# Gate and up of a gated MLP turned token-major, in eleven groups with two of eight weight pieces by seven products

## Chip, core and metric

The kernel runs on one core of a Trainium2 chip. The metric is the device time of one execution in microseconds (us). Engines: TensorE (PE in the profile; PEld its weight loads), VectorE (DVE), ScalarE (ACT), GpSimd (POOL) and SyncE (SP), which issues the loads.

## What is computed

One layer of a bidirectional encoder over 256 tokens with 2048 features: norm, two attention branches with gates, output projection, a gated MLP with a convolution of width 3 along the tokens, a gated per-layer embedding, norm. The part that matters here is the MLP, with 5632 inner columns:

```python
hf = rms_norm(x, ffn_norm[i])
g = dwconv_centred(hf @ w_ffn_gate[i], conv_w[i], conv_b[i])
x = x + (jax.nn.gelu(g) * (hf @ w_ffn_up[i])) @ w_ffn_down[i]
```

## The kernel before

**Precision.** Every fp32 operand of a product is split into a high half, rounded to fp32r, and a low half, the rest. A product is three matmuls (`thirds`, lines 361 to 366): high by high, high by low, low by high. The split of a weight is made on the chip: ScalarE rounds the raw weights (L263), VectorE subtracts (L264).

**Pieces and units.** The weights come in pieces of 128 x 2048 numbers, 1 MB each, in the order of use (`_pieces`); SyncE loads them into three buffers. `produce` cuts a piece into units of up to 1024 columns and splits them. There are rings for six plain units (`uh`, `ul`) and two units of differences (`vh`, `vl`); a new unit is made when the products that read an old one are issued (`drop`, `pump`), strictly in the order of `_UNITS`. So VectorE can be about two to three pieces ahead.

**Two ways to use a piece token-major.** In the stages B (branch gates), D (output projection), F (down) and G (embedding gate) the moving operand is weights, 128 x 512, and the stationary one 128 x 128 of activations. A piece holds two row blocks by two blocks of 512 columns; the activations are two row blocks by two halves of 128 tokens. A piece of kind `s` makes the eight products, 24 matmuls. A piece of kind `S` makes seven products, as in Winograd's form of Strassen's method, 21 matmuls. It needs two units of weight differences (T13 and T24; L256 to L258 make the differences on VectorE in the raw buffer, then they are split) and four sums of activations, made once per pair of row blocks (`sums_of`, L835 to L841). The products of an S piece come in the order M1, M7, M5, M6, M2, M3, M4; M7 and M5 need T13, M6 and M4 need T24. Each name is one of the eight PSUM banks; the eighth, P22, is used by s pieces and for transposes. `row_sums` joins the banks at the last piece of a stage: one copy on ScalarE and four adds of 512 columns on VectorE (L810 to L814), then for each of four blocks `finish`.

**Feature-major.** In E (gate and up) the weights are the stationary operand, 128 x 128, and the moving one is `hf`, 128 x 512: the high and low halves of 256 tokens. A block is a matmul of 512 (L307) and one of 256 with the low weights (L314), written as sixteen and sixteen (`unit_blocks`). There are 44 columns of 128 for gate and as many for up, half of them in E0 and half in E1. `mlp` (L962) does the rest for each column, on 128 x 256: the halves' sum (`gather`), the norm's scale, the three taps with a `tensor_scalar` and two `scalar_tensor_tensor` (L970 to L972), gelu by tanh, the product with up, the split of the result, and for five pairs of columns a half the sums for S pieces. The scale by the norm is a row spread over all partitions (`norm_columns`, one matmul).

**Stages.** E0, F00, F01, E1, F10, F11: F00 and F01 make the two halves of the 2048 output columns from E0's rows of activation, F10 and F11 from E1's. Each F stage has eleven pieces of the pattern `SsSsSsSsSss`, so F0 and F1 have 22 each. F's `finish` adds to the residual (L924, L926). In F11 the finished rows are turned back by transposes (`rows_pair`, L858) for the next stage, and two `combine` make activation sums. Behind F11 come pp0 and pp1 (one s piece each) and G.

**Order.** `at((stage, piece, product), f)` hangs work at a place of TensorE's program; the framework then orders the instructions of every engine with its own estimate of their times, mostly by their place in the program. Engines run their lists in order.

Of the kernel before, what the change touches and what calls it, by code (L numbers as in the profile page):

```python
# [16 lines left out]
P = 128  # L17
# [14 lines left out]
FC = FF // P  # L32
FHALF = FC // 2
EPS = 1e-6
# [53 lines left out]
WARM = 14  # L88
JOINT = 4
JOINED = 2  # L90
# [3 lines left out]
ALT = "SsSsSsSs"  # L94
DOWN = "SsSsSsSsSss"
FIRST_GATES = "ssssSsSs"


def _ffn(half):

    jobs = []
    for f in range(FHALF + 1):
        if f < FHALF:
            jobs.append(("g", half * FHALF + f))
        if f:
            jobs.append(("u", half * FHALF + f - 1))
    return jobs


def _pieces():  # L110
# [27 lines left out]
    for s in range(2):  # L138
        quads("D%d" % s, ("w_out", 2 * s * WIDE), ("w_out", (2 * s + 1) * WIDE), ALT)
    for half in range(2):  # L140
        names = {"g": "w_ffn_gate", "u": "w_ffn_up"}
        jobs = [(names[kind], f) for kind, f in _ffn(half)]
        joint = 0 if half else JOINT
        e = [(name, k, f) for k in range(KC) for name, f in jobs[:joint]]
        e += [(name, k, f) for name, f in jobs[joint:] for k in range(KC)]
        blocks("E%d" % half, e)
        for s in range(2):
            quads("F%d%d" % (half, s), ("w_ffn_down", 2 * s * WIDE), ("w_ffn_down", (2 * s + 1) * WIDE),
                  DOWN, half * FHALF)
    for s in range(2):  # L150
# [32 lines left out]
_EARLY = [0] + list(np.cumsum([_LAST_OF[u] + 1 for u in range(40)]))  # L183
RINGS = {"u": 6, "v": 2}


@with_exitstack
def _encoder(ctx: ExitStack, tc, xt, pt, xrow, cols, gainrow, table, onehot, mask, ident_in, wts, out):
# [9 lines left out]
    BANK = {"M2": 0, "M3": 1, "M4": 2, "M1": 3, "M7": 4, "M5": 5, "M6": 6, "P22": 7}  # L198
    RING = {"acc": (0, 1, 2), "sp": (3, 4), "pt": (5, 6), "misc": (7,), "e": (0, 1, 2, 3, 5, 6, 4)}
    turns = {"acc": 1}  # L200
# [241 lines left out]
    def gather(acc, scale=1.0, u=None, keep=lambda ins: ins):  # L442

        t = sc.tile([P, T], F32, name="t")
        keep(nc.scalar.activation(t, acc[:, T:], AF.Copy, scale=scale))  # L445
        if u is None:
            u = sc.tile([P, T], F32, name="u")
# [32 lines left out]
    def diagonal(r):  # L480

        dg = sc.tile([P, T], F32, name="rdg", bufs=1)
        for t in range(2):
            nc.vector.tensor_scalar(dg[:, t * P:(t + 1) * P], ident, r[:, t:t + 1], None, op0=ALU.mult)
        return dg

    def spread(key, dg):

        b = bank("misc", P, T)
        nc.tensor.matmul(b, ones, dg, start=True, stop=True)  # L490
        rt[key] = sc.tile([P, T], F32, name="rms", bufs=1)
        nc.scalar.activation(rt[key], b, AF.Copy)
# [337 lines left out]
    def sums_of(u, tag):  # L830

        tok = held["tok"]
        f = tok.tile([P, 4, P], F32, name="cmb")
        x11, x21, x12, x22 = (u[:, k, t * P:(t + 1) * P] for k in range(2) for t in range(2))
# [11 lines left out]
    def combine(key, m, pair, tag):  # L846

        u = held["tok"].tile([P, 2, T], F32, name="pair", bufs=2)
# [100 lines left out]
    residual("D1", 1, lambda k: held["merged"][:, k, :], "merged", True)  # L949
    for pair, which in enumerate(("M2", "M3", "M4", "P22")):  # L950
        at(("E0", 2 + pair), rows_pair, which, 4 + pair, hf, 1)

    def norm_columns():
        at(("E0", 11), spread, 1, diagonal(rows_root()))

    at(("E0", 8), norm_columns)

    def activation_row(k):
        k %= FHALF
        return held["act"][1][k - 16] if 16 <= k < 20 else held["act"][k // 20 * 2][:, k - k // 20 * 20, :]  # L960

    def mlp(kind, n, acc):  # L962
        tok = held["tok"]
        if kind == "g":
            if n % 2 == 0:
                held["gw"] = tok.tile([P, 4, T], F32, name="gw", tag="c%d" % (n // 2 % 2 + 1))
            c, w = (held["gw"][:, 2 * (n % 2) + i] for i in range(2))
            u = gather(acc)
            nc.vector.tensor_tensor(u, u, rt[1], op=ALU.mult)
            nc.vector.tensor_scalar(c, u, tap(1, n), tap(3, n), op0=ALU.mult, op1=ALU.add)  # L970
            nc.vector.scalar_tensor_tensor(c[:, 1:], u[:, :-1], tap(0, n), c[:, 1:], op0=ALU.mult, op1=ALU.add)
            nc.vector.scalar_tensor_tensor(c[:, :-1], u[:, 1:], tap(2, n), c[:, :-1], op0=ALU.mult, op1=ALU.add)  # L972
            nc.scalar.activation(w, c, AF.Square)
            nc.vector.tensor_scalar(w, w, 0.044715, 1.0, op0=ALU.mult, op1=ALU.add)
            nc.vector.tensor_tensor(w, w, c, op=ALU.mult)
            nc.scalar.activation(w, w, AF.Tanh, scale=GELU_C)
            nc.vector.scalar_tensor_tensor(c, w, 1.0, c, op0=ALU.add, op1=ALU.mult)
            held["gelu", n] = c
        else:
            if n % 2 == 0:  # L980
                held["pair"] = tok.tile([P, 2, T], F32, name="pair", bufs=2)
            u = gather(acc, u=held["pair"][:, n % 2])
            nc.vector.scalar_tensor_tensor(u, u, 0.5, rt[1], op0=ALU.mult, op1=ALU.mult)
            nc.vector.tensor_tensor(u, u, held.pop(("gelu", n)), op=ALU.mult)
            halves(activation_row(n), u)
            pair = n % FHALF // 2
            if n % 2 and DOWN[pair] == "S":
                combos["act", pair] = sums_of(held["pair"], pair // 2)

    ph_, pl_ = [], []  # L990

    def load_last():
        held["pr"] = held["tok"].tile([P, 2, T], F32, name="pair", bufs=2)
        keep(nc.sync.dma_start(held["pr"], pt))

    def split_last():
        for k in range(2):
            ph_.append(sc.tile([P, T], FR, name="t"))
            pl_.append(sc.tile([P, T], FR, name="u"))
            nc.scalar.activation(ph_[k], held["pr"][:, k], AF.Copy)  # L1000
            nc.vector.tensor_tensor(pl_[k], held["pr"][:, k], ph_[k].bitcast(F32), op=ALU.subtract)

    for half in range(2):
        held["act"] = [big.tile([P, 16, 2 * T], FR, name="act", tag="R1"),
                       [big.tile([P, 2 * T], FR, name="act1", tag="yb%d" % i) for i in range(4)],
                       held["tok"].tile([P, 2, 2 * T], FR, name="act2")]
        jobs = _ffn(half)
        joint = 0 if half else JOINT
        stage = "E%d" % half
        accs = [bank(which) for which in ("M1", "M5", "M6", "M7")[:joint]]  # L1010
        if joint:
            products(stage, lambda k: hf[:, k, :], KC, accs)
        for (kind, n), a in zip(jobs, accs):
            mlp(kind, n, a)
        turns["e"] = 0
        for kind, n in jobs[joint:]:
            mlp(kind, n, product(stage, lambda k: hf[:, k, :], KC, "e"))
        if half:
            at(("F10", 2, 0), load_last)
            at(("F10", 9, 0), split_last)  # L1020
            held["ssq"] = sc.tile([P, 2, 2], F32, name="ssq", bufs=1)
        residual("F%d0" % half, 0, activation_row, "act", half)
        if half:
            pl = big.tile([P, KC, 2 * T], FR, name="pl", tag="R0")
            for pair, when in enumerate((("F11", 0, 6), ("F11", 1, 2), ("F11", 1, 5), ("F11", 2, 1))):
                at(when, rows_pair, "P22", pair, pl, 2)
            at(("F11", 2, 4), combine, "pl", pl, 0, 0)
            at(("F11", 4, 4), combine, "pl", pl, 2, 1)
        residual("F%d1" % half, 1, activation_row, "act", half)
# [4 lines left out]
    gains = last[:, 2 * D:]  # L1034
    nc.sync.dma_start(gains, gainrow)
    for pair, which in enumerate(("M2", "M3", "M4", "P22")):
# [5 lines left out]
    at(("pp1", 0, 0), ple_root)  # L1042
    at(("pp1", 0, 4), combine, "pl", pl, 4, 2)
    at(("G0", 1, 4), combine, "pl", pl, 6, 3)
    names = ("M1", "M6", "M7", "M5")

    class Rows:
# [3 lines left out]
        def __getitem__(self, i):  # L1051
            c = i[1]
            h = (ph_, pl_)[c.start >= T][self.k]
            return h[:, c.start % T:c.start % T + P]

# [109 lines left out]
```

## Time and profile before

| | us |
|---|---|
| median of 3 runs (1457.73 to 1458.08) | 1457.87 |
| the profiled execution | 1458.43 |
| its span from first to last instruction | 1456.6 |
| E0, F0, E1, F1 of it | 247.1, 113.0, 244.9, 114.5 |

Loads move 282.88 MB, 194 GB/s on the mean. The page gives busy times by engine, the chain of waits that ended last, and groups of instructions by line. The windows table gives for each stretch its length and the busy time of each engine in it; the timeline lists instructions with start and duration, "x3" for three in a row, and in brackets how long the engine was idle before them and what ended that.

### The profile page before, as it was taken

Reading aid. Unit: us, or ns where it says so; the run is one execution under the profiler, and the core shown is the slowest. Engines: PE = TensorE matmul, PEld = TensorE weight load, DVE = VectorE, ACT = ScalarE, POOL = GpSimd, SP = SyncE. Lnnn points to the kernel's source line nnn. Section 1 sums busy time; section 2 is a strip of 40 time slices with the busy share of each in tenths; the row PEclk is TensorE's granted clock in tenths of the full one; section 3 lists DMA queues with packets and bytes.
Section 4 is the critical chain, followed back from the end, with each engine's and each line's share of the span. In section 5 each row is a group of like instructions: output and inputs, shape, how many; then the busy total and the mean of one; then the engine's idle time right before and its main releaser. Section 6 shows DMA issues by size and latency. Waiting matters only on the chain.

```text
span 1456.6 us, 19524 instructions
## 1 busy us (share of the span) xinstructions
PE 1445.2 (99%) x7488; PEld 1237.1 (85%) x7488; DVE 1248.2 (86%) x1841; ACT 824.1 (57%) x1149; POOL 4.9 (0%) x9
## 2 busy tenths in 40 slices
PE   9999999999999999999999999999999999999997
PEld 8888888888888888888888888888888888888785
DVE  7777665679998989989888899989888889999994
ACT  7555544546555656566555555455555555565763
POOL 0000000000000000000000000000000000000000
PEclk9999999999999999999999999999999999999999
DMA  9764445435456456465554545465555554546462
GB/s 319 259 205 152 148 170 175 174 143 202 187 192 233 185 204 238 177 231 190 188 200 175 202 149 224 173 257 182 201 181 195 182 195 172 191 193 249 156 233 85
DMA packets 46456, 282.88 MB, mean 194 GB/s; under 512 B 5076, under 2 KB 9812, under 8 KB 14108
## 3 DMA queue, kind: packets, MB, share of 16 engines
q1 hardware_dynamic: 45500, 280.46, 52.7%
q8 instruction: 58, 0.95, 0.3%
q10 hardware_dynamic: 864, 1.19, 0.2%
q14 instruction: 34, 0.28, 0.1%
HBM read 279.49 MB, written 2.14 MB: 193 GB/s over the span
## 4 chain that ended last, share of the span: by engine, by line
PE 98%; ACT 1%; issue 0%; DMA 0%; DVE 0%; POOLq 0%; POOL 0%; ACTq 0%; DVEq 0%
PE bank L307 29%; PE bank L314 15%; PE bank L364 14%; PE bank L365 14%; PE bank L366 14%; PE bank L291 2%; PE bank L353 2%; PE bank L355 2%; PE bank L354 2%; PE bank L292 1%; PE bank L858 1%; PE bank L675 0%; PE bank L623 0%; PE bank L622 0%; PE bank L621 0%
## 5 line engine op out<-in xcount | busy, mean ns | idle before, releaser
L263 ACT ACTIVATE uh<-raw 128x1024 fp32r<-128x1024 f32 (+2 forms) x518 | 522.1, 1017 | 402.2 <-PE bank L307 183.4
L264 DVE TENSOR_TENSOR ul<-raw,uh 128x1024 fp32r<-128x1024 f32 (+2 forms) x518 | 596.6, 1169 | 134.1 <-ACT uh L263 70.3
L307 PE MATMUL bank<-hf,uh 128*128 128x512 f32 x1408 | 336.4, 391 | 0.0
L307 PEld LDWEIGHTS bank<-hf,uh 128*128 128x128 f32 x1408 | 258.9, 188 | 50.2
L314 PEld LDWEIGHTS bank<-hf,ul 128*128 128x128 f32 x1408 | 180.4, 191 | 6.7
L314 PE MATMUL bank<-hf,ul 128*128 128x256 f32 x1408 | 182.8, 283 | 0.0
L263 ACT ACTIVATE vh<-raw 128x1024 fp32r<-128x1024 f32 x92 | 97.4, 1059 | 55.7 <-DVE raw L256 27.9
L264 DVE TENSOR_TENSOR vl<-raw,vh 128x1024 fp32r<-128x1024 f32 x92 | 111.8, 1218 | 0.4
L307 PE MATMUL bank<-hs,uh 128*128 128x512 f32 x432 | 103.6, 392 | 0.0
L445 ACT ACTIVATE t<-bank 128x256 f32<-128x256 f32 x122 | 46.5, 384 | 95.1 <-PE bank L314 89.7
L307 PEld LDWEIGHTS bank<-hs,uh 128*128 128x128 f32 x432 | 79.5, 188 | 15.6
L364 PE MATMUL bank<-uh,act 128*128 128x512 f32 x232 | 90.4, 390 | 0.0
L365 PE MATMUL bank<-ul,act 128*128 128x512 f32 x232 | 90.4, 390 | 0.0
L366 PE MATMUL bank<-uh,act 128*128 128x512 f32 x232 | 90.3, 389 | 0.0
L364 PE MATMUL bank<-uh,hs 128*128 128x512 f32 x172 | 67.3, 391 | 0.0
L366 PE MATMUL bank<-uh,hs 128*128 128x512 f32 x172 | 67.2, 391 | 0.0
L365 PE MATMUL bank<-ul,hs 128*128 128x512 f32 x172 | 67.1, 390 | 0.0
L256 DVE TENSOR_TENSOR raw<-raw 128x1024 f32<-128x1024 f32 x46 | 56.1, 1220 | 0.6
L314 PE MATMUL bank<-hs,ul 128*128 128x256 f32 x432 | 56.6, 284 | 0.0
L314 PEld LDWEIGHTS bank<-hs,ul 128*128 128x128 f32 x432 | 54.5, 191 | 1.0
L364 PE MATMUL bank<-vh,S 128*128 128x512 f32 x138 | 54.3, 398 | 0.0
L365 PE MATMUL bank<-vl,S 128*128 128x512 f32 x138 | 54.1, 392 | 0.0
(240 smaller groups left out, 2275.1 us busy)
## 6 DMA issues: line engine op xcount, KB each, us to landing
raw<-in_wts SPq DMA_DIRECT2D x251, 1024.0 KB, 4.8
raw<-in_wts SPq DMA_DIRECT2D x12, 512.0 KB, 7.3
xr<-in_xrow SPq DMA_DIRECT2D x4, 512.0 KB, 9.5
x<-in_xt SPq DMA_DIRECT2D x13, 128.0 KB, 6.5
hb<-hold SPq DMA_DIRECT2D x3, 514.0 KB, 7.5
hb<-hold SPq DMA_DIRECT2D x2, 768.0 KB, 7.4
last<-in_gainrow SPq DMA_DIRECT2D x1, 1024.0 KB, 4.9
out<-xr SPq DMA_DIRECT2D x4, 256.0 KB, 2.6
```

Of the source, the lines that this page charges most:

```text
L256: nc.vector.tensor_tensor(raw[:, :2 * WIDE], raw[:, WIDE:3 * WIDE], raw[:, :2 * WIDE], op=ALU.subtract)
L263: nc.scalar.activation(hi, src, AF.Copy)
L264: nc.vector.tensor_tensor(lo, src, hi.bitcast(F32), op=ALU.subtract)
L291: nc.tensor.matmul(acc, hi[:, w], m, start=first, stop=False, skip_group_check=True)
L307: nc.tensor.matmul(acc, weights(u)[0][:, o * P:(o + 1) * P], m, start=first, stop=False, skip_group_check=True)
L314: nc.tensor.matmul(acc[:, T:], weights(u)[1][:, o * P:(o + 1) * P], m[:, :T], start=False, stop=last, skip_group_check=True)
L353: nc.tensor.matmul(acc[:, :n * P], xh, hi, start=(k == 0), stop=False)
L354: nc.tensor.matmul(acc[:, :n * P], xh, lo, start=False, stop=False)
L364: nc.tensor.matmul(acc, sh, wh, start=first, stop=False)
L365: nc.tensor.matmul(acc, sh, wl, start=False, stop=False)
L366: nc.tensor.matmul(acc, sl, wh, start=False, stop=last)
L445: keep(nc.scalar.activation(t, acc[:, T:], AF.Copy, scale=scale))
```

## The change

E becomes token-major, with the same routines as F. It has 11 groups, E0 to E10, each of 512 columns of gate and the same 512 of up, eight pieces of the pattern `ssssSsSs`. Groups 0 to 5 belong to the first half of down, 6 to 10 to the second. The two S pieces of all groups use the sums of `hf`'s pairs 4 and 6, made once per half. `scaled` adds the banks and scales by the norm, one number a token, on ScalarE. `group_turns` hangs the rest into the next stage (the next group, or F00 or F10): for each pair of columns of gate, then of up, four transposes into one bank and a copy on ScalarE (`turned`), then `mixer` (taps, gelu) and `mixed` (product with up, split) on 128 x 512. In a group the banks are M1, M5, M6 and M7, free during the four s pieces; in F00 and F10 all four turns go through P22. Three of the five pairs of activation sums are made there, two `late` in the F stage. F's patterns become twelve pieces a stage in the first half and ten in the second. The gain rows' load is issued behind F11 instead of before pp0, the load of p in F10's seventh piece instead of its third. Smaller tiles move between pools to make room; those lines are left out of the diff.

```diff
-DOWN = "SsSsSsSsSss"
+MLP = "ssssSsSs"
+DOWN = ("SsSsSsSsSsss", "SsSsSsSsSs")
+MLP_GROUPS = (range(0, 6), range(6, 11))
...
-        blocks("E%d" % half, e)
+    for half, groups in enumerate(MLP_GROUPS):
+        for g in groups:
+            quads("E%d" % g, ("w_ffn_gate", g * WIDE), ("w_ffn_up", g * WIDE), MLP)
...
+HELD_TAGS = ({"act": (0, 1, 2, 3, 4), "next": (0, 1)}, {"act": (2, 3, 4, 0, 1), "next": (2, 3, 4, 0)})
...
-    for pair, which in enumerate(("M2", "M3", "M4", "P22")):
-        at(("E0", 2 + pair), rows_pair, which, 4 + pair, hf, 1)
-    def norm_columns():
-        at(("E0", 11), spread, 1, diagonal(rows_root()))
-    at(("E0", 8), norm_columns)
+    for pair, which, when in zip(range(4, 8), ("M1", "M5", "M6", "M7"), ((0, 4), (0, 7), (1, 2), (1, 5))):
+        at(("E0", *when), rows_pair, which, pair, hf, 1)
+    def rows_scale():
+        held["r1"] = rows_root()
+    mlp_pairs = [i for i, c in enumerate(MLP) if c == "S"]
+    at(("E0", 4, 0), rows_scale)
+    for pair, tag, when in zip(mlp_pairs, (3, 4), ((2, 4), (4, 4))):
+        at(("E0", *when), combine, "hf", hf, pair, tag)
...
-    def mlp(kind, n, acc):
...
+    def turned(which, n, pair, c):
+        p = bank(which, P, 2, T)
+        for k in range(2):
+            for t in range(2):
+                first = n * WIDE + pair * T + k * P
+                nc.tensor.transpose(p[:, k, t * P:(t + 1) * P], c[t][:, first:first + P], ident)
+        u = held["tok"].tile([P, 2, T], F32, name="ut" if n else "gt", bufs=1 if n else 2)
+        nc.scalar.activation(u, p, AF.Copy)
+        return u
+    def mixer(f, g):
+        c = held["tok"].tile([P, 2, T], F32, name="cc")
+        for k in range(2):
+            nc.scalar.activation(c[:, k], g[:, k], AF.Identity, scale=tap(1, f + k), bias=tap(3, f + k))
+            nc.vector.scalar_tensor_tensor(c[:, k, 1:], g[:, k, :-1], tap(0, f + k), c[:, k, 1:],
+                                           op0=ALU.mult, op1=ALU.add)
+            nc.vector.scalar_tensor_tensor(c[:, k, :-1], g[:, k, 1:], tap(2, f + k), c[:, k, :-1],
+                                           op0=ALU.mult, op1=ALU.add)
+        nc.scalar.activation(g, c, AF.Square, scale=math.sqrt(0.044715))
+        nc.vector.scalar_tensor_tensor(g, g, 1.0, c, op0=ALU.add, op1=ALU.mult)
+        nc.scalar.activation(g, g, AF.Tanh, scale=GELU_C)
+        nc.vector.scalar_tensor_tensor(c, g, 1.0, c, op0=ALU.add, op1=ALU.mult)
+        return c
+    def mixed(k, c, u):
+        nc.vector.scalar_tensor_tensor(u, u, 0.5, c, op0=ALU.mult, op1=ALU.mult)
...
+            nc.scalar.activation(d[:, :, :T], u, AF.Copy)
+            nc.vector.tensor_tensor(d[:, :, T:], u, d[:, :, :T].bitcast(F32), op=ALU.subtract)
+        if k // 2 in held["early"]:
+            combos["act", k // 2] = sums_of(u, held["early"][k // 2])
+    def group_turns(half, g, down, c):
+        k = 4 * (g - MLP_GROUPS[half][0])
+        stage = "F%d0" % half if down else "E%d" % (g + 1)
+        got = {}
+        def gate(which, pair):
+            got[pair] = turned(which, 0, pair, c)
+            if pair == 0:
+                got["c"] = mixer(4 * g, got[0])
+        def up(which, pair):
+            u = turned(which, 1, pair, c)
+            mixed(k + 2 * pair, got["c"], u)
+            if pair == 0:
+                got["c"] = mixer(4 * g + 2, got[1])
+        whens = ((0, 2), (0, 5), (1, 0), (1, 3)) if down else ((0, 3), (0, 6), (1, 1), (1, 5))
+        for f, pair, which, when in zip((gate, gate, up, up), (0, 1, 0, 1), ("M1", "M5", "M6", "M7"), whens):
+            at((stage, *when), f, "P22" if down else which, pair)
+    def late(pair, tag):
+        u = held["tok"].tile([P, 2, T], F32, name="ut")
+        for i in range(2):
+            row = activation_row(2 * pair + i).bitcast(F32)
+            nc.vector.tensor_tensor(u[:, i], row[:, :T], row[:, T:], op=ALU.add)
+        combos["act", pair] = sums_of(u, tag)
+    def scaled(t, n, a):
+        c = held["c"][t][:, cut[n]]
+        nc.vector.tensor_tensor(c, a, c, op=ALU.add)
+        nc.scalar.activation(c, c, AF.Copy, scale=held["r1"][:, t:t + 1])
...
+        for g in groups:
+            quads("E%d" % g, lambda k: hf[:, k, :], lambda i: combos["hf", i], scaled)
+            group_turns(half, g, g == groups[-1], held["c"])
+        for pair, tag in zip(pairs[3:], tags["act"][3:]):
+            at(("F%d0" % half, pair - 4, 4), late, pair, tag)
         if half:
-            at(("F10", 2, 0), load_last)
+            at(("F10", 6, 0), load_last)
             at(("F10", 9, 0), split_last)
+        else:
+            for pair, tag, when in zip(mlp_pairs, tags["next"], ((2, 4), (4, 4))):
+                at(("F01", *when), combine, "hf", hf, pair, tag)
...
-    nc.sync.dma_start(gains, gainrow)
+    at(("G0", 0, 0), lambda: keep(nc.sync.dma_start(gains, gainrow)))
```

More of the change, by code (lines that the diff above doesn't have):

```diff
@@ L994, in load_last @@
         keep(nc.sync.dma_start(held["pr"], pt))
     def split_last():
[L997 to L1003, printed above, removed]
+        ph, pl = (held["tok"].tile([P, 2, T], FR, name="pw", tag="gt", bufs=2) for _ in range(2))
@@ L1007, in _encoder @@
[L1007 to L1017, printed above, removed]
+                       held["tok"].tile([P, 4, 2 * T], FR, name="act2")]
```

84 lines of the change are left out of this document (25 added, 59 removed).

## The prediction

> **What bounds the kernel now.** I read the page first, for the engines' shares and the chain that ended last; then the windows table cut at the stage borders; then the timelines of TensorE and VectorE round those borders.
>
> ```profile
> PE 1445.2 (99%) x7488; PEld 1237.1 (85%) x7488; DVE 1248.2 (86%) x1841; ACT 824.1 (57%) x1149; POOL 4.9 (0%) x9
> PE 98%; ACT 1%; issue 0%; DMA 0%; DVE 0%; POOLq 0%; POOL 0%; ACTq 0%; DVEq 0%
> ```
>
> TensorE is busy for 99% of the span and makes 98% of the chain; VectorE is second with 86%. The windows say how close second is, stage by stage: the branch gates and projections, then E0, F0, E1, F1 (E: gate and up; F: both halves of down).
>
> ```profile
> 305.00:560.00 255.00, 255.00 (x1158) 210.51 (x1157) 238.06 (x300) 147.40 (x170) 0.00 (x0) 1.00 0.51 190
> ...
> 628.40:875.50 247.10, 247.10 (x1427) 218.42 (x1426) 219.47 (x394) 142.05 (x216) 0.71 (x1) 1.00 0.53 190
> 875.50:988.50 113.00, 113.00 (x501) 93.46 (x499) 103.02 (x116) 60.85 (x67) 0.00 (x0) 1.00 0.56 210
> 988.50:1233.40 244.90, 244.90 (x1409) 216.48 (x1408) 216.57 (x378) 136.35 (x203) 0.00 (x0) 1.00 0.52 187
> 1233.40:1347.00 113.60, 113.60 (x509) 93.80 (x507) 107.63 (x133) 66.60 (x80) 0.00 (x0) 1.00 0.57 212
> ```
>
> After the length come TensorE, weight loads, VectorE, ScalarE. TensorE is full everywhere at clock 1.00. VectorE is at 88% in E1, 95% in F1. The change takes matmuls from the first engine and gives work to the second, so both have to be counted.
>
> **TensorE's part.** Rows of its timeline: one round of gate and up, then the starts of F0, E1 and F1.
>
> ```profile
> 702.96 3.82 PE L307 MATMUL bank<-hf,uh 128*128 128x512 f32 x16
> 706.62 2.08 PE L314 MATMUL bank<-hf,ul 128*128 128x256 f32 x16
> ...
> 875.53 0.40 PE L364 MATMUL bank<-uh,act 128*128 128x512 f32 x1
> ...
> 988.50 3.79 PE L307 MATMUL bank<-hf,uh 128*128 128x512 f32 x16
> ...
> 1233.40 0.40 PE L364 MATMUL bank<-uh,act 128*128 128x512 f32 x1
> ```
>
> A weight piece of gate or up is one such round, 16 blocks high and 16 low; E1 is 44 of them, (1233.40 - 988.50) / 44 = 5.566 us. Removed: 88 x 5.566 = 489.8 us. F0 has 22 pieces, 10 of seven products (21 matmuls) and 12 of eight (24): 498 matmuls in 988.50 - 875.53 = 112.97 us, 0.2268 us each. The new groups are made of the same matmuls: six pieces of 24 and two of 21, 186 a group, 2046 in all. Added: 464.1 us. In what follows an S piece (seven products) lasts 4.76 us, an s piece (eight) 5.44, a product 0.68. F keeps its 996 matmuls; 48 of them go from F1 to F0.
>
> Turning back: 16 transposes a group, 176 in all. Four of them in F1:
>
> ```profile
> 1300.69 0.39 PE L364 MATMUL bank<-vh,S 128*128 128x512 f32 x1
> 1300.92 0.60 PE L858 MATMUL bank<-ident,xr 128*128 128x128 f32 x4
> 1301.28 0.48 PE L365 MATMUL bank<-vl,S 128*128 128x512 f32 x1
> 1301.60 0.39 PE L366 MATMUL bank<-vh,S 128*128 128x512 f32 x1
> ```
>
> From 1300.69 to 1301.60 lie two matmuls (0.454) and four transposes: 0.456, so 0.114 each. Added: 20.1 us. The norm's spread matmul goes: -0.2, as for a product of one matmul. TensorE alone: 464.1 + 20.1 - 489.8 - 0.2 = -5.8 us.
>
> **VectorE's part.** When its instructions follow each other without waiting they start closer than their durations, so I take starts:
>
> ```profile
> 1240.80 2.35 DVE L264 TENSOR_TENSOR vl<-raw,vh 128x1024 fp32r<-128x1024 f32 x2
> 1243.07 3.08 DVE L264 TENSOR_TENSOR ul<-raw,uh 128x1024 fp32r<-128x1024 f32 x3
> ...
> 1288.57 1.88 DVE L924 TENSOR_TENSOR xr<-xr,bank 128x512 f32<-128x512 f32 x3
> 1290.37 1.22 DVE L926 TENSOR_TENSOR xr<-xr,c 128x1024 f32<-128x1024 f32 x1
> ...
> 1311.33 0.28 DVE L835 TENSOR_TENSOR cmb<-pair 128x128 f32<-128x128 f32 x1
> 1311.54 0.28 DVE L836 TENSOR_TENSOR cmb<-pair 128x128 f32<-128x128 f32 x1
> ...
> 1361.00 1.70 DVE L462 SCALAR_TENSOR_TENSOR pl<-bank,cl,pl 128x256 fp32r<-128x256 f32 x4 [0.15 <-ACT pl L461]
> 1362.62 1.21 DVE L264 TENSOR_TENSOR ul<-raw,uh 128x1024 fp32r<-128x1024 f32 x1
> ```
>
> 1024 columns: (1243.07 - 1240.80) / 2 = 1.14 us; 512: (1290.37 - 1288.57) / 3 = 0.60; 128: 0.20; 256 with a tap: (1362.62 - 1361.00) / 4 = 0.40. So the weights of an s piece cost 2.28; those of an S piece 1.74 plain, and 4.62 for the differences and their low halves, 6.36 in all. The mixer of two columns costs 4 x 0.40 + 2 x 0.60 = 2.8, the product with up 1.2: 8.0 a group. Row sums and adds cost 8 x 0.60 = 4.8; one piece's seven-product sums of activations 4 x 0.20 + 0.60 = 1.4, a late one 2.1 with its two adds.
>
> A group then asks 6 x 2.28 + 2 x 6.36 + 8.0 + 4.8 = 39.2 us of VectorE, or 40.6 with a set of sums, against 186 x 0.2268 + 16 x 0.114 = 44.0 of TensorE. That is 89 to 92%, no more than 305 to 560 us carries today (238.06 / 255 = 93%) with TensorE full. Inside the E stages I therefore charge no stall. ScalarE holds 136.35 of 244.90 in E1, 25 us a group; 19 more would be needed before it counts.
>
> The trouble is F. A group's mixers run in the next stage, so those of the last group of each half fall into F00 and F10, with two late sums each: 8.0 + 4.2 us. Before, F1 starts with only the last column's leftovers. Walk through F10. A group's last two pieces last 10.2 us and ask 6.36 + 2.28 + 4.8 = 13.4, so F10 starts 3.2 us behind. Until the fourth product of its fifth piece, which needs the second difference, VectorE owes 3.2 + 6.36 + 2.28 + 8.0 + 6.36 + 2.1 = 28.3 us. TensorE gets there after 2 x (4.76 + 5.44) + 1.8 (transposes) + 3 x 0.68 = 24.2. It waits 4.1 us. By the seventh piece the sums are 39.0 and 34.4, 4.6 us; by the ninth the gap shrinks. The same walk fits F00. The same sum for before is 17.4 to 19.7; the trace has 19.3, and room:
>
> ```profile
> 1251.47 1.22 DVE L264 TENSOR_TENSOR vl<-raw,vh 128x1024 fp32r<-128x1024 f32 x1
> ```
>
> ```profile
> 1255.87 0.39 PE L364 MATMUL bank<-vh,S 128*128 128x512 f32 x1
> ```
>
> The difference is ready at 1252.69, 19.3 us into F10, and wanted 3.2 us later. In F11 there is no room already:
>
> ```profile
> 1300.48 1.21 DVE L264 TENSOR_TENSOR vl<-raw,vh 128x1024 fp32r<-128x1024 f32 x1
> ```
>
> ```profile
> 1301.82 0.40 PE L364 MATMUL bank<-vh,S 128*128 128x512 f32 x1
> ```
>
> Ready at 1301.69, used at 1301.82. The new F10 ends with one s piece after its last S instead of two: 5.44 us of TensorE's time are gone and only 2.28 us of VectorE's. F11 waits 3.2 us.
>
> Stalls: 4.6 + 4.6 + 3.2 = 12.4 us. If the order on TensorE is written so that the two products which don't need the difference go first (1.4 us), each is that much less: 8.2. A reason for less than that, down to zero, is that mixers could be put behind weights: nothing before the ninth piece of F10 or F00 reads their rows. I take 10.3, the middle, because the check against before came out within 1 us.
>
> Edits that I cost at nothing: the r1 root on GpSimd, asked at E0's fifth piece and used at its eighth; the row turns of E0, same number in other banks; the p load, moved from F10's third piece to its seventh, with two pieces left to land. The gain rows' load moves behind F11. Today it stands in SyncE's queue before weight loads:
>
> ```profile
> 1332.42 0.33 SPq L1035 DMA_DIRECT2D last<-in_gainrow  x1
> ```
>
> ```profile
> 1340.67 2.01 ACT L263 ACTIVATE uh<-raw 128x1024 fp32r<-128x1024 f32 x2 [6.05 <-DMA raw<-in_wts]
> ```
>
> ScalarE lost 6.05 us there, TensorE none. What comes free helps VectorE to meet the first difference of the stage behind F11, which also has 3.2 us less: I set the two against each other.
>
> Sum on the profiled execution (1458.43 us, 1456.6 of span and 1.8 round it): -5.8 + 10.3 = +4.5. The median of the runs is 0.56 lower, 1457.87, so 1462.4 us; with stalls of 8.2 to 12.4 it is 1460.3 to 1464.5, and the 1 to 2 us by which the walk through before came out give 1459 to 1467. As a check, VectorE's sum from E0 to F11 is 11 x 39.2 + 6 x 1.4 + 4 x 2.0 (sums of the normed rows) for gate and up, 20 x 6.36 + 24 x 2.28 = 182 for the weights of down, and some 48 for its sums and turns: 677 us, in 714 of TensorE, 95%. At the 93.4% of 305 to 560 us it would take 725, a stall of 11.
>
> **The rivals.** *The order hides it.* Mixers slip behind weights on VectorE, F00 and F10 keep their pace, and only F11's last us or two remain. For it: F1 runs today at 107.63 of 113.60 with TensorE full, and the walk can't see the planner. Against it: mixers are earlier in the program than those weights. The time is 1457.87 - 5.8 = 1452.1, up to 1455 with F11's part: faster. It holds if VectorE's debt at F10's fifth piece is under 24 us instead of 28. Chance 0.27. *Half of it*: stalls of 3 to 7 us: 1455 to 1459, chance 0.12.
>
> *Full durations.* The mixers are chains, each operation waiting for the one before, and then a start costs the duration. Rows of E1 and F0:
>
> ```profile
> L971 DVE SCALAR_TENSOR_TENSOR gw<-u,cl,gw 128x255 f32<-128x255 f32 x22 | 10.6, 482 | 0.7
> ```
>
> ```profile
> L258 DVE TENSOR_TENSOR raw<-raw 128x512 f32<-128x512 f32 x9 | 6.2, 687 | 0.1
> ```
>
> With 1.22 (L264 above), 0.69, 0.48 and 0.28 a group asks 43.4 us, 45.2 with sums: 1.2 over TensorE's 44.0 in six groups, 7 us. The walk through F00 and F10, done again with these, gives 9.9 each, F11 about 5: 32 us, 1484. Half way from the forecast it is 1473. Chance 0.13 for anything from 1468 on. The Trainium skill has this as a rule, in "VectorE: DVE Perf Modes", section "The DRAIN you can't avoid": the next operation does not start until the pipe has emptied, though one that nothing holds starts earlier. Of the two the trace agrees with the second: two of 1.22 us in 2.35.
>
> **How the numbers follow.** The forecast, 1459 to 1467, has 0.48. A measurement of this kernel can tell about 0.2%, 2.9 us: faster is under 1455.0, slower over 1460.8. Faster is the first rival, 0.27. The same is half of it, 0.12, and the lowest quarter of the forecast, 0.12: 0.24. The rest is slower, 0.49. The range runs from the first rival's bottom, 1451.8, to 1471 where the last one begins; about 0.15 lie outside.
>
> **What would show it.** Right: 2046 matmuls of 128x512 in E at 0.227 us, transposes at 0.11, VectorE about 90% in E and 97% or more in F00, F10 and F11; TensorE idle in front of products with a difference (its line for sums, waiting for the low halves of weights) in the fifth and seventh piece of F00 and F10, and in F11. Wrong: TensorE full through F10, then the first rival holds; or gaps inside the E groups, in front of transposes or of their S pieces, then the chains cost more than starts say. A transpose that costs nearer its duration would add to every group alike.

## The result, and the profile after

The changed kernel takes 1470.47 us (median of 5, 1468.65 to 1472.92) against 1457.87 for the kernel before beside it (1457.73 to 1458.43). The ratio is 1.0087, with a 95% interval of 1.0073 to 1.0101: slower, by about 12.6 us. The profiled execution is the longest of the five, 1472.92 us with a span of 1471.1, so it is 14.5 us over the profiled execution of before.

The page's row of engines and its chain, after:

```profile
PE 1449.0 (98%) x6892; PEld 1203.7 (82%) x6892; DVE 1292.3 (88%) x1720; ACT 885.9 (60%) x1188; POOL 4.9 (0%) x9
PE 88%; DVE 7%; ACT 2%; DMA 1%; issue 1%; POOL 0%; POOLq 0%; ACTq 0%; DVEq 0%
```

TensorE still fills 98% of the span, yet its part of the chain fell from 98% to 88%, and VectorE makes 7%. The windows, cut at the new stage borders (E0 to E5, F0, E6 to E10, F1, pp, and G to its last matmul), columns as before:

```profile
628.40:894.40 266.00, 265.58 (x1214) 218.46 (x1213) 250.58 (x329) 178.08 (x238) 0.71 (x1) 1.00 0.51 189
894.40:1023.70 129.30, 127.57 (x563) 103.08 (x562) 124.18 (x160) 75.08 (x91) 0.00 (x0) 1.00 0.54 205
1023.70:1243.75 220.05, 219.09 (x995) 180.67 (x994) 200.70 (x251) 142.54 (x183) 0.00 (x0) 1.00 0.49 185
1243.75:1360.90 117.15, 111.01 (x480) 87.69 (x479) 113.78 (x157) 71.63 (x95) 0.00 (x0) 0.97 0.48 181
1360.90:1373.60 12.70, 12.70 (x65) 10.55 (x64) 12.08 (x16) 11.36 (x19) 0.00 (x0) 1.00 0.43 168
1373.60:1461.40 87.80, 86.08 (x377) 69.64 (x376) 75.64 (x108) 48.48 (x73) 2.00 (x2) 1.00 0.45 169
```

VectorE works 94% of E0 to E5, 96% of F0, 91% of E6 to E10 and 97% of F1. F1 has more than half of TensorE's idle time in this table (6.14 of 10.97 us), and it alone has a granted clock below 1. E got shorter, 486.0 us instead of 492.0. F0 and F1 together got 19.0 longer, though they have no matmul more but the transposes.

To separate work from waiting I count TensorE's instructions in each stage, at 0.2268 us for a matmul of 512 columns, 0.120 for one of 256 and 0.112 for a transpose. What is left of the stage's length is waiting (or a lower clock):

| length, of it waiting (us) | before | after | e3 below | e9 below |
|---|---|---|---|---|
| E, both parts | 492.0, 1.8 | 486.0, 4.1 | 485.6, 3.6 | 483.1, 1.2 |
| F0 | 113.0, 0.0 | 129.3, 3.7 | 126.4, 0.8 | 127.0, 1.4 |
| F1 | 114.5, 0.2 | 117.1, 11.9 | 107.9, 0.9 | 107.9, 0.9 |
| pp | 14.2, 1.1 | 12.8, 0.1 | 12.8, 0.1 | 12.8, 0.1 |
| G to the start of its last matmul | 84.4, 0.3 | 87.4, 2.8 | 85.1, 1.0 | 85.2, 1.0 |
| sum of waiting | 3.4 | 22.6 | 6.4 | 4.6 |

TensorE's work from E0 on fell from 814.6 to 810.1 us, and its waiting grew by 19.2: -4.5 + 19.2 = 14.7, against 14.5 measured. The largest single wait stands at the border of F10 and F11. TensorE's and VectorE's timeline of the changed kernel there:

```profile
1299.38 0.39 PE L352 MATMUL bank<-uh,act 128*128 128x512 f32 x1
1301.13 0.50 PE L350 MATMUL bank<-uh,act 128*128 128x512 f32 x1 [1.36 <-ACT uh L249]
...
1301.63 1.22 DVE L250 TENSOR_TENSOR ul<-raw,uh 128x1024 fp32r<-128x1024 f32 x1
...
1302.76 1.21 DVE L250 TENSOR_TENSOR vl<-raw,vh 128x1024 fp32r<-128x1024 f32 x1
...
1303.90 0.68 DVE L797 TENSOR_TENSOR c<-bank,c 128x512 f32<-128x512 f32 x1
...
1304.72 0.77 PE L350 MATMUL bank<-vh,S 128*128 128x512 f32 x1 [3.09 <-DVE c L797]
1305.29 0.63 PE L351 MATMUL bank<-vl,S 128*128 128x512 f32 x1
```

Counted from the end of a matmul at full pace (0.227 us behind its start), TensorE waits 1.5 us for a rounded weight, issues one matmul, and waits 3.4 us for a bank that VectorE must read first (L797, the row sums of F10); the brackets, counted from the modelled ends, say 1.36 and 3.09. VectorE is not idle: it works off weights and comes late. The rounded weight is late by the same cause. ScalarE's rounding waited for its load:

```profile
1300.45 0.63 ACT L249 ACTIVATE uh<-raw 128x512 fp32r<-128x512 f32 x1 [0.70 <-DMA raw<-in_wts]
```

The last load ahead of it was issued at 1295.38, after 3.1 us in which SyncE waited for VectorE to be done with the buffer (L250, 1294.14 to 1295.36). So what VectorE owes reaches TensorE in two ways: by its own results, and by loads that start late because VectorE frees their buffers late. Behind the second wait the matmuls start 0.43 us apart. Windows of the same stretch:

```profile
1290.00:1299.40 9.40, 9.40 (x43) 7.65 (x42) 9.40 (x12) 6.80 (x9) 0.00 (x0) 1.00 0.64 237
1299.40:1304.70 5.30, 0.87 (x3) 0.19 (x2) 5.30 (x7) 2.88 (x4) 0.00 (x0) 0.84 0.17 39
1304.70:1310.00 5.30, 5.28 (x13) 4.18 (x14) 5.30 (x9) 1.06 (x1) 0.00 (x0) 0.51 0.90 369
1310.00:1320.00 10.00, 9.95 (x46) 7.79 (x44) 7.86 (x9) 6.77 (x10) 0.00 (x0) 1.00 0.00 2
```

VectorE is busy in all of the first three windows. In the third the granted clock is 0.51: twelve matmuls lose 0.2 us each, 2.4 us on top of the wait.

### The profile page after: what moved, and what is told of

It is laid out like the page before. It is cut to its first block, busy times and chain, and to the rows that moved or that the text cites. A ratio compares the mean times of both kernels' runs of the same rounds, so it can differ in the third digit from the quotient of the medians.

```text
span 1471.1 us, 18240 instructions
## 1 busy us (share of the span) xinstructions
PE 1449.0 (98%) x6892; PEld 1203.7 (82%) x6892; DVE 1292.3 (88%) x1720; ACT 885.9 (60%) x1188; POOL 4.9 (0%) x9
## 4 chain that ended last, share of the span: by engine, by line
PE 88%; DVE 7%; ACT 2%; DMA 1%; issue 1%; POOL 0%; POOLq 0%; ACTq 0%; DVEq 0%
PE bank L351 22%; PE bank L352 22%; PE bank L350 22%; PE bank L293 7%; PE bank L300 4%; DVE ul L250 3%; PE bank L277 2%; PE bank L339 2%; PE bank L341 2%; PE bank L340 2%; DVE vl L250 1%; PE bank L956 1%; PE bank L278 1%; DMA raw<-in_wts 1%; ACT uh L249 1%
## 5 line engine op out<-in xcount | busy, mean ns | idle before, releaser
L249 ACT ACTIVATE uh<-raw 128x1024 fp32r<-128x1024 f32 (+2 forms) x518 | 507.5, 995 | 355.5 <-DMA raw<-in_wts 129.1
L250 DVE TENSOR_TENSOR ul<-raw,uh 128x1024 fp32r<-128x1024 f32 (+2 forms) x518 | 583.0, 1146 | 101.1 <-ACT uh L249 81.8
L350 PE MATMUL bank<-uh,hf 128*128 128x512 f32 x572 | 226.4, 396 | 0.6 <-DVE c L1021 0.6
L352 PE MATMUL bank<-uh,hf 128*128 128x512 f32 x572 | 223.3, 390 | 0.0
L351 PE MATMUL bank<-ul,hf 128*128 128x512 f32 x572 | 222.8, 389 | 0.0
L249 ACT ACTIVATE vh<-raw 128x1024 fp32r<-128x1024 f32 x136 | 143.1, 1056 | 59.1 <-DVE raw L242 33.2
L250 DVE TENSOR_TENSOR vl<-raw,vh 128x1024 fp32r<-128x1024 f32 x136 | 165.0, 1219 | 2.5 <-ACT vh L249 2.1
L352 PEld LDWEIGHTS bank<-uh,hf 128*128 128x128 f32 x572 | 107.3, 188 | 23.1
L350 PEld LDWEIGHTS bank<-uh,hf 128*128 128x128 f32 x572 | 107.4, 188 | 22.4 <-issue 1.3
L351 PEld LDWEIGHTS bank<-ul,hf 128*128 128x128 f32 x572 | 107.6, 188 | 21.2
L350 PE MATMUL bank<-vh,S 128*128 128x512 f32 x204 | 79.7, 405 | 5.4 <-DVE c L797 3.1
L242 DVE TENSOR_TENSOR raw<-raw 128x1024 f32<-128x1024 f32 x68 | 82.9, 1220 | 0.5
L351 PE MATMUL bank<-vl,S 128*128 128x512 f32 x204 | 80.9, 396 | 0.6 <-DVE vl L250 0.6
L352 PE MATMUL bank<-vh,S 128*128 128x512 f32 x204 | 79.6, 393 | 0.0
```

Source lines behind the costliest of these rows:

```text
L242: nc.vector.tensor_tensor(raw[:, :2 * WIDE], raw[:, WIDE:3 * WIDE], raw[:, :2 * WIDE], op=ALU.subtract)
L249: nc.scalar.activation(hi, src, AF.Copy)
L250: nc.vector.tensor_tensor(lo, src, hi.bitcast(F32), op=ALU.subtract)
L350: nc.tensor.matmul(acc, sh, wh, start=first, stop=False)
L351: nc.tensor.matmul(acc, sh, wl, start=False, stop=False)
L352: nc.tensor.matmul(acc, sl, wh, start=False, stop=last)
```

## The experiments

Theory 1: VectorE enters F00 and F10 in debt through the last group's mixers and the late sums, F's patterns leave no time to repay, and the debt is called in wherever TensorE next needs VectorE. Rivals: weight loads are late behind the load of p (theory 2); the chain from sums to product, or VectorE's share over the whole MLP, does it. The kernel before, beside the first four, took 1458.25 us; beside the next four 1458.44; beside the last two 1458.31.

**e1: the last group's mixers left out.**

```diff
-                got["c"] = mixer(4 * g, got[0])
+                got["c"] = got[0] if down else mixer(4 * g, got[0])
...
-                got["c"] = mixer(4 * g + 2, got[1])
+                got["c"] = got[1] if down else mixer(4 * g + 2, got[1])
```

> Left out: the three taps and the gelu of the last group of each half (512 of the 5632 gate columns twice), so its rows are gate times up alone. This takes 8.0 us of VectorE work from the first two pieces of each half's first down stage and leaves the 2046 products, the transposes and all transfers. Theory 1 (VectorE enters F00 and F10 in debt through the last group's two mixers and cannot repay it at 97% busy): the 3.7 us of idle TensorE in F00 shrink to under 1, the 4.9 us at the border of F10 and F11 and the 2.3 us of lower clock behind it go: 1457 to 1462 us. Theory 2 (the queue of weight loads, held up by the load of p, starves the F stages): F1 stays at 117 us, time 1467 to 1471. Theory 3 (the chain from last sum to next product, whatever VectorE owes): no change, 1469 to 1473.

1461.47 us, ratio 1.002 (1.0011 to 1.0029). Windows of F0 and F1:

```profile
894.30:1020.40 126.10, 126.09 (x564) 103.68 (x563) 118.62 (x148) 72.01 (x83) 0.00 (x0) 1.00 0.56 211
1239.30:1348.20 108.90, 106.89 (x479) 86.25 (x478) 108.17 (x145) 67.41 (x87) 0.00 (x0) 1.00 0.51 194
```

F0 has no waiting left to speak of, F1 loses 8 of its 12 us, and its clock is 1.00. VectorE's work fell by 5.6 us in each of them (124.18 to 118.62, 113.78 to 108.17), not by 8.0 as expected, since the product with up stayed. So 9 of the 12.6 us hang on the mixers, 11 us of VectorE's work in these two places. The edit takes ScalarE's part of the mixers away too (75.08 to 72.01 us, 71.63 to 67.41), so e1 alone does not say which engine it is; e5 does. G, behind F1, waits 3.7 us here instead of 2.8.

**e2: the load of p on GpSimd's queue.**

```diff
-        keep(nc.sync.dma_start(held["pr"], pt))
+        keep(nc.gpsimd.dma_start(held["pr"], pt))
```

> The load of p is issued by GpSimd instead of SyncE, so no weight load stands behind it. Theory 2 (weights late behind the load of p): the stall of 4.9 us at the border of F10 and F11 goes, with the 2.3 us of lower clock after it: 1462 to 1466 us. Theory 1 (VectorE's debt): at most 1 us changes, 1469 to 1472 us, and F11's first product still waits for row sums.

1472.68 us, ratio 1.0097 (1.008 to 1.0114). The border in its timeline:

```profile
1301.37 0.50 PE L350 MATMUL bank<-uh,act 128*128 128x512 f32 x1 [1.15 <-ACT uh L249]
1305.15 0.76 PE L350 MATMUL bank<-vh,S 128*128 128x512 f32 x1 [3.27 <-DVE c L797]
```

The same wait at the same place with the same releaser. Theory 2 falls, though the time is 0.7 us above the range given for theory 1, and F1 waits 14.5 us instead of 11.9; why is not known. Weight loads do come late, but behind VectorE and not behind p: in the changed kernel the first one behind p's waits 4.1 us for VectorE to be done with its buffer.

**e4: one S piece a group in E instead of two** (`MLP = "ssssssSs"`).

> Gate and up with one S piece of eight instead of two: 33 more products (+7.5 us of TensorE), 11 fewer S pieces of splits (about 45 us less VectorE in the E stages). The F stages are as they were. Theory 1 (the debt arises in F00 and F10 themselves): only the 3.7 us of stalls inside E go, 1473 to 1477 us. Rival (VectorE's share of the whole MLP, 93 to 95%, carried from group to group, makes the stalls): E hands over with nothing owed and most of the 19 us of stalls go: 1459 to 1464 us.

1476.06 us, ratio 1.0122 (1.0107 to 1.0137). The two parts of E:

```profile
628.00:896.62 268.62, 268.62 (x1231) 222.21 (x1230) 227.50 (x294) 169.00 (x225) 0.70 (x1) 1.00 0.51 187
1025.30:1247.25 221.95, 221.95 (x1011) 183.63 (x1009) 182.05 (x227) 134.67 (x173) 0.00 (x0) 1.00 0.51 184
```

VectorE has 85% and 82% of E now, and the waiting in E falls from 4.1 to 1.1 us. F0 and F1 still wait 3.1 and 12.2. So the rival that puts the waits down to VectorE's share over the whole MLP falls. Whether E's last group hands something over is not tested by this, because e4 keeps the last S piece of each group, and VectorE reaches F10 in the same state. Its last addition of the group's row sums, in the changed kernel and in e4:

```profile
1248.52 0.68 DVE L1021 TENSOR_TENSOR c<-bank,c 128x512 f32<-128x512 f32 x1
```

```profile
1251.94 0.69 DVE L1021 TENSOR_TENSOR c<-bank,c 128x512 f32<-128x512 f32 x1
```

F10 starts at 1243.75 and at 1247.25, so that is 4.8 us into it and 4.7. What VectorE gained earlier in E did not reach F.

**e5: the late sums left out.**

```diff
+    def repeat(pair, other):
+        combos["act", pair] = combos["act", other]
...
-        for pair, tag in zip(pairs[3:], tags["act"][3:]):
-            at(("F%d0" % half, pair - 4, 4), late, pair, tag)
+        for pair in pairs[3:]:
+            at(("F%d0" % half, pair - 4, 4), repeat, pair, pairs[2])
```

The last two S pieces of each half use the third one's sums again.

> Left out: the late sums of each half's last two S pieces (they multiply the sums of the third S piece again). This takes two times 2.1 us of VectorE work from F00 and from F10 and nothing else; the mixers of the last group stay. Theory 1 in its full form (mixers and late sums together are the debt): 1461 to 1465 us, the 4.9 us at the border of F10 and F11 shrink to about 1 and the lower clock behind it goes. Rival (the mixers alone: what comes after the first two pieces falls into slack): 1468 to 1471 us.

1463.58 us, ratio 1.0037 (1.0023 to 1.0051). F0 and F1:

```profile
894.80:1021.40 126.60, 126.60 (x564) 103.38 (x563) 120.35 (x146) 74.42 (x89) 0.00 (x0) 1.00 0.56 210
1240.00:1352.70 112.70, 109.28 (x480) 87.28 (x478) 110.04 (x143) 70.47 (x93) 0.00 (x0) 0.98 0.50 188
```

VectorE's work falls by 3.8 and 3.7 us, two thirds of e1's relief, and gives three quarters of its gain. ScalarE's work falls by 0.7 and 1.2 us only, so it is VectorE's that counts. Either part suffices for F0; G waits 4.0 us. What TensorE waited for in F00 of the changed kernel (the wait at 930.81 us, shown further down) is a rounded weight whose load came late:

```profile
922.71 1.22 DVE L250 TENSOR_TENSOR vl<-raw,vh 128x1024 fp32r<-128x1024 f32 x1
...
923.99 0.33 SPq L229 DMA_DIRECT2D raw<-in_wts  x1
...
929.70 1.06 ACT L249 ACTIVATE uh<-raw 128x1024 fp32r<-128x1024 f32 x1 [1.90 <-DMA raw<-in_wts]
```

SyncE issued the load as soon as VectorE was done with the buffer at 923.93, and ScalarE waited for it until 929.70. ScalarE's copy of a late sum stands ahead of this weight in its list and had waited 5.11 us for VectorE, but it was over 1.90 us before the load landed, so it did not set the time.

**e6: four S pieces in the second half, S first as before** (`DOWN` for that half `SsSsSsSsss`).

> Second half with four S pieces instead of five, the S first as in the changed kernel (SsSsSsSsss): +1.4 us of TensorE, -9.2 us of VectorE, one late sum fewer, F10 ends with three s pieces. If the sum of VectorE work in the half decides (105 us against 108): the border stall and the lower clock behind it go, F00 stays with its 3.7 us: 1463 to 1467 us. If the order decides (S ahead of the mixers): F10's stalls stay, 1469 to 1473 us.

1461.69 us, ratio 1.0023 (1.0014 to 1.0033), 1.3 us under the expected range. F1:

```profile
1241.40:1351.80 110.40, 109.64 (x486) 86.77 (x485) 108.03 (x144) 69.05 (x91) 0.00 (x0) 1.00 0.54 205
```

F1's waiting goes from 11.9 to 3.8 us, and G's from 2.8 to 0.7, which was not in the expectation. A shorter wait in F1 alone does not do that: in e1 and e5 F1 waits less than in the changed kernel and G more (3.7 and 4.0 us). G waits about 1 us or less in the runs with four S pieces a stage in the second half, and 2.6 to 4.4 in those with five; why was not tried.

**e3: small pieces first, and four S pieces in the second half.** With s pieces first, all four of their banks are in use at once, so the last group's turns and the row turns of pl must move out of P22.

```diff
-DOWN = ("SsSsSsSsSsss", "SsSsSsSsSs")
+DOWN = ("ssSsSsSsSsSs", "ssSsSsSsSs")
...
-        whens = ((0, 2), (0, 5), (1, 0), (1, 3)) if down else ((0, 3), (0, 6), (1, 1), (1, 5))
+        whens = (0, 3), (0, 6), (1, 1), (1, 5)
...
-            at((stage, *when), f, "P22" if down else which, pair)
+            at((stage, *when), f, which, pair)
...
-            for pair, tag, when in zip(mlp_pairs, tags["next"], ((2, 4), (4, 4))):
+            for pair, tag, when in zip(mlp_pairs, tags["next"], ((4, 4), (6, 4))):
...
-            for pair, when in enumerate((("F11", 0, 6), ("F11", 1, 2), ("F11", 1, 5), ("F11", 2, 1))):
-                at(when, rows_pair, "P22", pair, pl, 2)
-            at(("F11", 2, 4), combine, "pl", pl, 0, tags["next"][0])
-            at(("F11", 4, 4), combine, "pl", pl, 2, tags["next"][1])
+            for pair, which, when in zip(range(4), ("M1", "M5", "M6", "M7"), ((0, 6), (1, 1), (1, 3), (1, 6))):
+                at(("F11", *when), rows_pair, which, pair, pl, 2)
+            at(("F11", 4, 4), combine, "pl", pl, 0, tags["next"][0])
+            at(("F11", 6, 4), combine, "pl", pl, 2, tags["next"][1])
```

> The down stages start with two s pieces, the second half has four S pieces instead of five (3 more products in each of its 2 stages: +1.4 us of TensorE, -9.2 us of VectorE), the last group's turns and the row turns of pl use the four product banks instead of P22, and the combinations of hf and pl in F01 and F11 start two pieces later. Theory 1: the mixers now meet pieces of 2.3 us of VectorE work against 3.9 us of TensorE, the debt is repaid before the first S: F00 126 to 127 us, F1 107 to 109, time 1456 to 1461 us. Theory 2 (queue of loads): the loads and their order are the same in number, F1 stays over 115: 1468 to 1473 us.

1458.76 us, ratio 1.0006 (0.9996 to 1.0015): level with the kernel before. F0 and F1:

```profile
894.57:1020.96 126.39, 126.39 (x563) 103.69 (x562) 124.91 (x159) 75.53 (x91) 0.00 (x0) 1.00 0.53 201
1240.82:1348.80 107.98, 107.98 (x490) 88.42 (x489) 107.03 (x142) 69.28 (x93) 0.00 (x0) 1.00 0.50 190
```

F0 keeps VectorE's work (124.91 against 124.18 us) and its five S pieces and still loses 2.9 of its 3.7 us of waiting, so there the order and the banks gain. How much is less sure: with F0 as in the changed kernel, e2, e4 and e6 wait 2.4, 3.1 and 2.3 us in it. VectorE stands at 99% in both, and TensorE waits for almost nothing.

**e7: e3 with five S pieces in the second half** (`ssSSsSsSSs`).

> The third kernel (small pieces first, 1458.8 us) with five S pieces in the second half again (ssSSsSsSSs): -1.4 us of TensorE, +9.2 us of VectorE there. If the sum decides: VectorE had 107 us of work in 108 us of F1, so it becomes the bound and F1 takes 115 to 117 us: 1465 to 1468 us. If the order decides: 1456 to 1459 us.

1468.57 us, ratio 1.0071 (1.0055 to 1.0086), 0.6 us above the range expected if the sum decides. F1:

```profile
1241.00:1355.10 114.10, 110.05 (x483) 86.35 (x482) 113.05 (x154) 71.15 (x96) 0.00 (x0) 1.00 0.45 165
```

VectorE is at 99% of F1 again, but F1 is 6.2 us longer than in e3, and pp and G together 3.6. In the second half the sum of VectorE's work decides, and the order helps little. F1 came out a little shorter than expected, and G waits 4.4 us.

One window from the start of F1 to the end of the span shows the same, for the changed kernel, e5, e1, e6, e3 and e7 (each from its own profile):

```profile
1243.75:1471.10 227.35, 209.81 (x919) 167.88 (x917) 205.22 (x288) 133.94 (x192) 2.93 (x3) 0.97 0.47 177
```

```profile
1239.97:1464.10 224.13, 208.29 (x919) 167.49 (x917) 201.53 (x274) 132.71 (x190) 2.93 (x3) 0.98 0.48 179
```

```profile
1239.32:1459.50 220.18, 206.04 (x919) 166.60 (x917) 199.77 (x276) 129.55 (x184) 2.93 (x3) 0.99 0.49 182
```

```profile
1241.39:1460.50 219.11, 208.10 (x925) 167.10 (x923) 195.97 (x271) 130.75 (x187) 2.92 (x3) 0.98 0.49 184
```

```profile
1240.82:1456.70 215.88, 206.18 (x925) 168.18 (x923) 196.77 (x271) 130.74 (x188) 2.92 (x3) 0.98 0.49 181
```

```profile
1241.03:1466.70 225.67, 210.16 (x919) 167.43 (x917) 206.12 (x287) 134.22 (x193) 2.93 (x3) 0.98 0.46 172
```

VectorE's 205.22, 201.53, 199.77 and 195.97 us go with lengths of 227.35, 224.13, 220.18 and 219.11, the last with 1.4 us more matmuls: 0.9 to 1.3 us for each of VectorE's. At equal work the order is worth 3.2 us (e6 to e3) or 1.7 (changed to e7); the two kernels with 9 us more of VectorE's work are 8 and 10 us longer than those with less.

**e8: e3 with the activation sums on GpSimd**, the additions of `sums_of` (L822 to L825 in its listing) and `late` (L1017) for `act` alone; one of five lines changed alike:

```diff
-        nc.vector.tensor_tensor(f[:, 0], x21, x22, op=ALU.add)
+        eng.tensor_tensor(f[:, 0], x21, x22, op=ALU.add)
```

> The third kernel (1458.8 us) with the sums of activation pairs (nine times four additions of 128 columns, and three late ones) on GpSimd instead of VectorE: about 10 us less VectorE work over the MLP. If VectorE's load still costs the third kernel its last 2 to 5 us: 1454 to 1457 us. If the additions on GpSimd slow VectorE, or hold the tile that the mixers need: 1460 to 1470 us.

1478.66 us, ratio 1.014 (1.0125 to 1.0155), beyond the worse branch. Groups from E0 to pp, GpSimd's first, then VectorE's step behind them:

```profile
L1017 POOL TENSOR_TENSOR ut<-act 128x256 f32<-128x256 f32 x6 | 9.8, 1653 | 160.3 <-DVE act L987 101.4 <-DVE act L443 58.8
L824 POOL TENSOR_TENSOR cmb<-cmb,ut 128x128 f32<-128x128 f32 x9 | 7.3, 809 | 0.2
...
L828 DVE TENSOR_TENSOR S<-cmb,S 128x512 fp32r<-128x512 f32 x15 | 10.3, 690 | 15.3 <-ACT S L827 15.3
```

An addition of 128 columns takes up to 0.81 us there, against 0.28 on VectorE, and one of 256 takes 1.65 against 0.42. The subtraction that needs the sums stayed in VectorE's list, and VectorE stood in front of it for 15.3 us. The work left the busy engine, the waiting came to it. Nor did much leave: VectorE's busy time from E0 to F11 fell from 681.75 us (e3) to 679.23, where about 10 us less was expected; why is not known. The Trainium skill, "GPSIMD Engine Reference", section "1. Specifications", names GpSimd's SBUF interfaces as shared with VectorE; its opening has VectorE about twice as fast for elementwise work. Here, beside a VectorE busy for 88 to 96% of the stages, it was two to four times, with 0.55 us for the quickest of the four lines of 128 columns. No run here shows whether the shared interfaces are the reason.

**e9 and e10: e3 with the pieces of E in another order**, `sssSssSs` and `sssSsSss`.

> The third kernel (1458.8 us) with the pieces of gate and up in the order sssSssSs instead of ssssSsSs; the same products, so the same TensorE work. In the E stages the third kernel still has 3.6 us that are not matmuls at full pace. If they come from the two differences standing close together, three pieces between them give back up to 2.5 us: 1456 to 1458 us. If the first difference then meets the mixers of the group before, it costs: 1460 to 1466 us.

> The third kernel with the order sssSsSss: both differences one piece earlier, two s pieces at the end of each group, so row sums and turns of a group meet less weight work. If the end of a group is what costs in E: 1456 to 1458 us. If the mixers at its head are: 1460 to 1468 us.

e9 takes 1456.76 us, ratio 0.9992 (0.9983 to 1.0001); e10 1460.15, ratio 1.0013 (1.0004 to 1.0021). e9's E:

```profile
628.85:893.46 264.61, 264.61 (x1214) 218.81 (x1212) 247.57 (x326) 177.16 (x238) 0.70 (x1) 1.00 0.53 196
1020.45:1238.98 218.53, 218.53 (x995) 180.80 (x994) 199.11 (x251) 140.75 (x183) 0.00 (x0) 1.00 0.52 192
```

With three s pieces in front of the first S piece and two between the two, instead of four and one, E's waiting goes from 3.6 to 1.2 us. With both differences moved ahead (e10) and one s piece between them again it is 6.4, 1.3 of it in one wait at the border of two groups, for a bank that VectorE has still to read (L1021); whether it is the mixers that make VectorE late there was not tried. e9 is 13.7 us faster than the changed kernel, and its interval still takes in the kernel before.

## Why the prediction was right in sign and 8 us short

The time lies above the forecast of 1459 to 1467 us, in the part that was given to the rival of full durations with a chance of 0.13. On the profiled execution the sum was -5.8 of work and 10.3 of stalls, +4.5; the traces show -4.5 and 19.2. Of the 8.9 us of stalls too few, 5.1 are in F0 and F1 (15.4 instead of 10.3), 2.3 in E and 1.5 in pp and G.

*TensorE's part* held. Matmuls start 0.227 us apart, and a transpose costs 0.112 us (with the small gap behind each turn). The saving in work is 4.5 us instead of 5.8, because the 5.566 us for a removed column held some of E's old waiting (1.8 us in all).

*VectorE's price by starts* held, and with it the rival of full durations falls, although its time came nearest. E6 to E10 hold the weights of five groups but the mixers of four, since E10's run in F10. Their VectorE instructions are 103 of 1024 columns, 104 of 512, 32 of 255 with a tap and 12 of 128. At the prediction's prices that is 195.0 us by starts (1.14, 0.60, 0.40, 0.20) and 216.1 by full durations (1.22, 0.69, 0.48, 0.28). VectorE was busy for 200.70 us, 3% over the first and 7% under the second. Mixers in F10:

```profile
1253.13 0.87 DVE L966 SCALAR_TENSOR_TENSOR cc<-gt,cl,cc 128x255 f32<-128x255 f32 x2
1253.92 0.87 DVE L968 SCALAR_TENSOR_TENSOR cc<-gt,cl,cc 128x255 f32<-128x255 f32 x2
1254.71 0.68 DVE L244 TENSOR_TENSOR raw<-raw 128x512 f32<-128x512 f32 x1
1255.31 1.22 DVE L250 TENSOR_TENSOR ul<-raw,uh 128x1024 fp32r<-128x1024 f32 x1
1256.45 0.68 DVE L971 SCALAR_TENSOR_TENSOR gt<-gt,cc 128x512 f32<-128x512 f32 x1
```

Two taps take 0.79 us from start to start, 0.40 each, as forecast. The steps of the mixer stand apart in the list, with weights between them, so the chain costs little.

*"Inside the E stages I therefore charge no stall"* was 2.3 us wrong (4.1 of waiting instead of 1.8); e4 and e9 speak for VectorE, meeting two S pieces too close together. The average of 91 to 94% hid it.

*F00, 4.6 us*: 3.7. The place was the seventh piece alone; the fifth passed without a wait. TensorE's timeline there, 35 us into F00:

```profile
929.21 0.39 PE L352 MATMUL bank<-uh,S 128*128 128x512 f32 x1
930.81 0.73 PE L350 MATMUL bank<-uh,act 128*128 128x512 f32 x2 [1.21 <-ACT uh L249]
931.76 0.73 PE L350 MATMUL bank<-vh,S 128*128 128x512 f32 x2 [0.22 <-ACT vh L249]
```

That the size came out is partly luck. The walk had TensorE wait for the low half of a difference; the longest wait here, 1.4 us from the end of a matmul at full pace, is for a rounded plain weight whose load started late. The walk had no term for loads.

*F10 and F11, 4.6 and 3.2 us, less what a reordered TensorE saves* is the step that failed. The two stages waited 9.5 us, where the walk had at most 7.8, and 2.4 more were lost to the clock, for which it had no term. The rival's mechanism was half there: as the rows of mixers above show, their steps did slip behind weights, and F10's fifth piece passed without a wait. But slipping only moves a debt. It came due at the border of F10 and F11, as 1.5 and 3.4 us with one matmul between, 4.9 together, where the walk had 3.2; and the longer one was for row sums and not for a difference. The walk let each stage start again with its own 3.2 us; in the trace F1 has VectorE at 97% and never gets even.

*"I set the two against each other"*, the gain rows' load against the shorter end of F11, was wrong by 2.5 us: G waits 2.8 us. It is not VectorE's work in F1 alone that sets this: e1 asks 108.17 us there and G waits 3.7, e6 asks 108.03 and G waits 0.7. pp gave 1.0 back.

*"I take 10.3, the middle"*: the reason given for the lower half, that TensorE's order could spare 1.4 us a stall, concerned single waits and not the sum of work. The check by VectorE's whole share (a stall of 11) told little, since e4 freed 42 us of that share (451.3 to 409.6 us) in E, and F waited as before.

One reading was slightly off: the rows at 1255.87 and 1301.82 us (L364) read the rounded half of the difference. The low half is read by the L365 behind them, 0.23 us later, so the room was 3.4 and 0.4 us. That changes nothing in the sum.

## What to carry to other kernels

When work moves to the second-busiest engine, keep its balance stage by stage, with what it owes at each border, and carry the debt on: an order that lets urgent work pass only postpones it to the next place where the queue must be empty. Price the debt where it falls due, here with one long wait instead of several short ones. Count loads among what a late engine holds up, if it is the last reader of their buffers. Moving a helper's additions to a third engine helps only if no step behind them stays in the busy engine's list.

## What was not expected of the hardware

A wait of TensorE can cost more than its length. In the changed kernel, e2 and e4, waits of 4.9 us with one matmul in between were followed by 12, 14 and 13 matmuls 0.43 us apart instead of 0.227. After waits of 1.2 and 1.6 us with one matmul between (e5) there were 8, and after 1.3 and 0.9 us in G of e7 there were 9. Windows of e5:

```profile
1290.00:1297.50 7.50, 5.08 (x22) 3.68 (x21) 7.49 (x10) 5.60 (x6) 0.00 (x0) 1.00 0.47 179
1297.50:1302.50 5.00, 5.00 (x16) 3.89 (x16) 5.00 (x9) 1.69 (x2) 0.00 (x0) 0.66 0.92 388
```

After single waits of 1.2 to 1.4 us (e1 at 1294 us, the changed kernel at 931) the clock stayed at 1.00, and in e2 at 1291 even after 0.4 and 1.7 us with one matmul between. In e8 at 940, 1.7 and 2.9 us with five matmuls between were followed by only about six slow ones. So the loss does not follow from the sum of the waits alone. The Trainium skill, "TensorE: Matmul & The Clock Gate", section "What's actually happening", says that the clock halves after an idle window of about 3.4 us, in windows that run freely, and comes back after a busy one. The halving agrees (0.43 against 0.227 us); e5 and e7 show that 2.9 and 2.2 us of waiting with one or two matmuls inside can be enough.

The runs of the changed kernel and of e3 and e9 scatter by 4 to 6 us, those of before by 1 to 2. What varies from run to run was not found.
